# Reordering the operands, gates and reads of the output block products in a hybrid encoder layer

## The chip, the cores and the metric

The kernel runs on one core of a Trainium2 chip. The metric is the time on the device in microseconds (us), the median of several runs; less is better. The core has five engines with queues of their own: TensorE (PE, matrix products; PEld is its loading of weights), VectorE (DVE), ScalarE (ACT), GpSimd (POOL), and SyncE (SP), which issues most of the DMAs. Each engine works through its queue in order; between engines there are semaphores.

## What is computed

One layer of an encoder over 2048 tokens of width 1024, in float32. An input projection feeds two mixers: gated linear attention and latent attention with softmax, each with an output of width 512. What matters here is the end:

```python
    o_a = gla_branch(...)                       # (2048, 512), gated
    o_b = mla_branch(...)                       # (2048, 512), ends in o * silu(gate)
    mixed = concatenate([o_a, o_b], -1) @ w_out # (2048, 1024)
    x = layer_norm(ALPHA * x + mixed, ln_g, ln_b)
```

## The kernel before

Every product of float32 matrices is made of three matmuls (`mm3`, line 445): each operand is split into a high part, a copy rounded by ScalarE (`hi`, L393), and a low part, the difference, subtracted by GpSimd or VectorE (`lo`, L399). So each operand tile costs one ScalarE copy and one subtraction before TensorE can use it; the third matmul of a group is the first to need the low part.

The stages follow one another: the input projection with the linear attention, then softmax attention in 16 blocks (4 heads by 4 blocks of 512 queries), then the output projection of 16 chunks of 128 tokens. The tail of the attention is interleaved with chunks 0 to 5. The last attention block's output is made at the very end of that: TensorE's product `y` (L1802) in the bank "o" of PSUM, the copy `yc` of it to SBUF by ScalarE (L1807), and a store to DRAM (L1808); `rows` (L1784) copies and stores the reciprocals of the softmax sums.

Chunks 6 and 7 are plain products (8 k-tiles by 2 halves by 3, 48 matmuls each). Chunk 7 writes to the banks "o" and "ap". Chunks 8 to 15 are taken in four **pairs** of row blocks with seven block products instead of eight (class `Pair`, L1966): the activations of two chunks form the four blocks A11, A12 (row 0) and A21, A22 (row 1), and sums of them S1 = A21 + A22, S3 = A11 - A21, S2 = S1 - A11, S4 = A12 - S2. S2 and S4 overwrite A11, S3 overwrites A21, so S2 must wait until the split of A11 is done. The products are P1 (A11), P5 (S1), P6 (S2), P3 (S4), P7 (S3), P2 (A12), P4 (A22), twelve matmuls each, in this order on four PSUM banks 0, 1, 2, 3, 0, 1, 3; the last pair has P2 ahead of P7 and P4 in two halves. The second factors of P5 to P7 and, from the pairs on, of P4 are sums of blocks of w_out that were stored earlier and are fetched by `fetch_t` ("1h" to "4l"); "4h" and "4l" are four loads each (L2209).

The steps of a pair, each with its engine:

- `load` (L1979, SyncE): four DMAs per row: the linear attention's output to `of[:, 0]`, the gate and the softmax reciprocals to the buffer `gr`, the softmax attention's output to `of[:, 1]`. There is one buffer `gr` for even and one for odd chunks, shared by all pairs. Odd pairs take the two SBUF tiles `lng` and `lnb` as `of`, which held the norm's weights until `ln_psum` (L2196) has copied them to PSUM; even pairs take tiles "xf".
- `load_res` (L1994, SyncE): the residual row from `x`.
- `gate` (L1999, GpSimd): two multiplications per row, on the softmax half (A12 of row 0, A22 of row 1).
- `add` (L2007, VectorE), `hi` (ScalarE), `lo` (GpSimd): the operands.
- `copy` c1, c7 (ScalarE, L2036) and `sum` U2, U3 (VectorE, L2040): P1, and later P7, added to bank 2.
- `read` (VectorE, L2043): R1, R5, R5b, R2, R6, R3, R7, R4, R4b add banks to the two output rows; a product's bank is free for the next one after its reads.
- for row 0 `squares` and `scale` (ScalarE) and `centre` (VectorE, L2079, waits for the squares); for row 1 `stats` and `finish_a` (VectorE, with `rsqrt` on ScalarE); then `finish_b` for both (VectorE L2328, and the stores L2329). In the last pair row 0 ends on ScalarE and GpSimd (`finish_first`), which reads `lnbc`, a copy of the norm's bias (`copy_lnb`, L2083, ScalarE).

The order is written out by hand. `Pair.put` gives each step a place in time; the places are sorted, and `in_order` chains the instructions of all five engines in that sorted order. The places stand in `PLACE_PAIR` (L135), relative to T, the planned start of the pair's first product: T = 21.76 + 19.05 p for pair p, on a clock that begins with chunk 6. `load`, `res` and `gate` hold values for rows 0 and 1. `read_last` holds the last pair's places. The tables `put(place, fn)` of chunks 6 and 7, of `rows` (6.5), `yc` (6.51), `ln_psum` (2.0 and 3.5) and of `fetch_t` (1.0; 21.9 and 21.91) stand in `attention` (L1939 to L1963). So a step is moved past another by a change of its place alone, on its engine's queue only.

Of the kernel before, what the change touches and what calls it, by code (L numbers as in the profile page):

```python
# [80 lines left out]
    max=1.21,  # L81
    sub=(9.47, 8.65, 7.39, 7.37, 7.49, 6.63, 6.95, 7.44),
    exp=(10.18, 9.95, 7.63, 9.15, 8.26, 9.12, 7.84, 8.01),
    hi=(10.39, 10.41, 9.81, 10.32, 9.82, 10.74, 10.53, 10.47),
    lo=(11.99, 11.22, 11.21, 12.62, 11.98, 11.51, 10.87, 10.63),
# [22 lines left out]
    hi=(10.43, 11.83, 12.21, 14.39, 15.18, 22.96, 28.7, 34.03),  # L108
    lo=(15.35, 16.07, 20.38, 20.41, 24.45, 25.82, 33.5, 36.25),
# [9 lines left out]
    gate=(-20.72, -12.46, -4.41, 43.92),  # L119
# [14 lines left out]
PAIR0, PAIR_US = 8, 19.05  # L134
PLACE_PAIR = dict(  # L135
    load=(-31.0, -31.5),
    res=(-10.0, -8.0),
    gate=((-19.94, -18.58), (-24.72, -21.3)),
    add=dict(S1=-10.55, S3=-9.85, S2=-9.15, S4=-4.37),
    hi=dict(A11=-17.26, S1=-9.75, S2=-8.35, A12=-5.39, S3=-4.77, S4=-3.53, A22=-2.66),  # L140
    lo=dict(A11=-13.14, S1=-8.45, S2=-7.09, S3=-3.67, A22=1.77, A12=3.13, S4=4.49),
    product=dict(P1=0.0, P5=2.72, P6=5.44, P3=8.16, P7=10.88, P2=13.6, P4=16.32),
    last=dict(P1=0.0, P5=2.72, P6=5.44, P3=8.16, P2=10.88, P7=13.6, P4=16.32),
    gate1=((-14.6, -13.3), (-19.95, -18.6)),
    read=dict(c1=2.78, R1=5.9, R5=6.5, R5b=7.1, U2=10.61, R2=11.24, R6=11.87, c7=14.91, U3=15.63, R3=16.26, bn22=16.89,
              R7=17.52, sq=18.25, R4=20.34, R4b=20.97, bn21=21.6, rs=21.9, fa=(21.7, 22.23), fb=(23.9, 26.7)),
    read_last=dict(c1=2.78, lnb=3.5, R1=5.0, R5=6.3, R5b=6.9, U2=8.9, R2=9.5, R3=10.1, R4b=10.7, R6=11.5, bn12=12.1,
                   R7=14.1, bn11=14.7, R3p=16.9, R4p=17.5, bn22=18.1, fa=(15.3, 20.2), fb=(17.0, 20.3)),
)

# [61 lines left out]
    lo=(-0.5, 0.357),  # L212
# [79 lines left out]
    lo=(-0.452, -1.813),  # L292
# [65 lines left out]
    lo=(-0.124, 0.045),  # L358
# [24 lines left out]
class K:  # L383
# [819 lines left out]
    def sweep_c(self):  # L1203


        with ExitStack() as ctx:
# [17 lines left out]
            for n in SETUP_C:  # L1224
                put(n, 0, getattr(self, "su_" + n))
            for s in steps:
                for n in range(8):
                    put("pz", s["st"], self.c_pz, s, n, j=n)
                for n in STEP_C:
                    put(n, s["st"], getattr(self, "c_" + n), s)  # L1230
# [735 lines left out]
class Pair:  # L1966
# [128 lines left out]
    def put(self, put, T, last):  # L2095
        at = lambda place, fn, *a: put(T + place, fn, *a)
        P_, op = PLACE_PAIR, self.op
        if self.p:
            for r in (1, 0):
                at(max(P_["load"][r], 4.9 - T if self.p == 1 else -99) - 0.01 * r, self.load, r)  # L2100
        for r in range(2):
            at(P_["res"][r], self.load_res, r)
            for n in range(2):
                at(P_["gate1" if self.p == 1 else "gate"][r][n], self.gate, r, n)
        for n in self.OPERANDS:
            if n[0] == "S":
                at(P_["add"][n], self.add, n)
            at(P_["hi"][n], self.hi, n)
            at(-2.2 if n == "S4" and not self.p else P_["lo"][n], self.lo, n)
        bank = [lambda i=i: op.pw[i] for i in range(4)]  # L2110
        t = P_["last" if last else "product"]
        b = dict(P1=0, P5=1, P6=2, P3=3, P7=1 if last else 0, P2=0 if last else 1, P4=3)
        for n in t:
            if not (last and n == "P4"):
                at(t[n], self.product, n, bank[b[n]])
        e = P_["read_last" if last else "read"]
        at(e["c1"], self.copy, bank[0])
        at(e["U2"], self.sum, bank[2])
        if last:
            reads = (("R1", 0, 0, 0), ("R5", 1, 1, 1), ("R5b", 0, 1, 1), ("R2", 0, 1, 2), ("R3", 1, 1, 2), ("R4b", 1, 0, 2),  # L2120
                     ("R6", 0, 1, 3), ("R7", 0, 0, b["P2"]), ("R3p", 1, 1, b["P7"]), ("R4p", 1, 0, b["P7"]))
        else:
            at(e["c7"], self.copy, bank[b["P7"]])
            at(e["U3"], self.sum, bank[2])
            reads = (("R1", 0, 0, 0), ("R5", 1, 1, 1), ("R5b", 0, 1, 1), ("R2", 0, 1, 2), ("R6", 0, 1, 3), ("R3", 1, 1, 2),
                     ("R7", 0, 0, b["P2"]), ("R4", 1, 0, 3), ("R4b", 1, 0, 2))
        for n, r, h, x in reads:
            at(e[n], self.read, r, h, bank[x])
        if not last:
            at(e["bn22"], self.stats, 1, 1, 1)  # L2130
            at(e["bn21"], self.stats, 1, 0, 0)
            at(e["sq"], self.squares, 0)
            at(e["rs"], self.scale, 0)
            at(e["fa"][0], self.centre, 0)
            at(e["fa"][1], op.finish_a, self.rows[1])
            for r in range(2):
                at(e["fb"][r], op.finish_b, self.rows[r])
            return
        at(e["lnb"], self.copy_lnb)
        at(e["bn12"], self.stats, 0, 1, 1)  # L2140
        at(e["bn11"], self.stats, 0, 0, 0)
        at(e["bn22"], self.stats, 1, 1, 2, 3)
        for i, x in enumerate((3, 0)):
            cs, half = slice(256 * i, 256 * i + 256), lambda x=x: bank[x]()[:, :256]
            at(t["P4"] + PAIR_US / 14 * i, self.product, "P4", half, cs)
            at(t["P4"] + PAIR_US / 14 * (i + 1) + 0.45, self.read, 1, 0, half, cs)
            at(t["P4"] + PAIR_US / 14 * (i + 1) + 0.46, self.stats, 1, 0, i, 3, cs)
        at(e["fa"][0], op.finish_a, self.rows[0])
        at(e["fb"][0], self.finish_first)
        at(e["fa"][1], op.finish_a, self.rows[1])  # L2150
        at(e["fb"][1], op.finish_b, self.rows[1])
# [246 lines left out]
```

## Time and profile before

| | us |
|---|---|
| median of 3 runs | 1290.94 |
| the runs | 1290.94, 1289.06, 1290.98 |
| the profiled execution | 1290.68 |
| its span, first to last instruction | 1288.9 |
| outside of the span | 1.8 |

| engine | busy us | share of the span |
|---|---|---|
| PE | 1257.7 | 98% |
| DVE | 949.8 | 74% |
| ACT | 873.8 | 68% |
| POOL | 847.7 | 66% |

Times in rows of the profile are counted from the start of the span. A timeline row reads: start, duration, engine, line of the program, operation, tiles out<-in, shapes, count; in brackets the idle time of the engine ahead of it and what ended it. TensorE's rows overlap: a matmul begins before the one ahead of it has left the array, so the step from start to start is its price, not the duration. A row of a stretch (windows) reads: the stretch, its length, the busy time of PE, PEld, DVE, ACT and POOL with the number of instructions, the granted TensorE clock as a share of full speed, the mean share of time that the 16 DMA engines worked, and GB/s. Chunk 6 and 7 and the four pairs fill the stretch from 1172 us to the end.

### The profile page before, as it was taken

How to read it: one execution, taken by the hardware profiler on the slowest of the kernel's cores; microseconds unless marked ns; L12 is line 12 of the kernel's file. 1: busy time of each engine (PE TensorE's matmuls, PEld its weight loads, DVE VectorE, ACT ScalarE, POOL GpSimd, SP SyncE). 2: the span in 40 equal slices, each digit the busy share in tenths (PEclk: the TensorE clock that was granted, in tenths of full speed). 3: DMA queues.
4: the chain of work that ended last, by engine and by line, in shares of the span. 5: the costliest groups of instructions: out<-in, count | busy, mean ns of one | idle time of the engine just before them, and what ended most of it. 6: DMA issues, size and time to landing. Idle time of an engine off the chain costs nothing.

```text
span 1288.9 us, 20174 instructions
## 1 busy us (share of the span) xinstructions
PE 1257.7 (98%) x6928; PEld 1109.6 (86%) x6928; DVE 949.8 (74%) x1706; ACT 873.8 (68%) x1549; POOL 847.7 (66%) x546
## 2 busy tenths in 40 slices
PE   7999999999999999999999999999999999998996
PEld 7999999999889999999788888888888888887875
DVE  7865775555675455555798888888888889558897
ACT  7765657666676656655688888888888888623444
POOL 0245555453567666671288888889999999955771
PEclk9999999999999999999999999999999999999999
DMA  8332525253665565565501111122223212468951
GB/s 297 99 91 62 182 69 172 83 154 100 212 228 179 179 208 181 188 211 167 146 1 41 42 42 41 42 58 58 61 69 103 55 42 73 156 186 313 326 196 66
DMA packets 122518, 166.81 MB, mean 129 GB/s; under 512 B 18502, under 2 KB 71118, under 8 KB 121776
## 3 DMA queue, kind: packets, MB, share of 16 engines
q1 hardware_dynamic: 114256, 163.39, 39.9%
q0 software_dynamic: 768, 2.10, 0.5%
q8 instruction: 55, 0.90, 0.3%
q10 hardware_dynamic: 7392, 0.03, 0.3%
q14 instruction: 47, 0.39, 0.2%
HBM read 106.72 MB, written 58.75 MB: 128 GB/s over the span
## 4 chain that ended last, share of the span: by engine, by line
PE 75%; DVE 6%; ACT 5%; DMA 4%; POOL 3%; issue 2%; SPq 0%; DVEq 0%; POOLq 0%; ACTq 0%
PE o L447 4%; PE o L448 4%; PE o L449 4%; PE pS L1633 4%; PE pS L1634 4%; PE pS L1635 4%; PE pS L1636 4%; PE pS L1637 4%; PE ipa L447 3%; PE ipa L449 3%; PE ipa L448 3%; PE pz L448 2%; PE pz L449 2%; PE pz L447 2%; PE ipg L447 2%
## 5 line engine op out<-in xcount | busy, mean ns | idle before, releaser
L399 POOL TENSOR_TENSOR pl<-s,ph 128x1024 fp32r<-128x1024 f32 x128 | 306.4, 2418 | 56.3 <-ACT ph L393 56.3
L1655 DVE TENSOR_TENSOR rm<-pS,rm 128x512 f32<-128x512 f32 x210 | 144.8, 690 | 26.5 <-ACT s L1642 20.9
L1679 DVE TENSOR_TENSOR s<-s,mb 128x1024 f32<-128x1024 f32 x128 | 151.2, 1213 | 9.4 <-PE mb L1673 9.3
L1642 ACT ACTIVATE s<-pS 128x1024 f32<-128x1024 f32 x128 | 131.3, 1026 | 37.7 <-PE pS L1637 33.3
L393 ACT ACTIVATE ph<-s 128x1024 fp32r<-128x1024 f32 x128 | 135.0, 1057 | 13.5 <-PE o L449 12.9
L1683 ACT ACTIVATE s<-s 128x1024 f32<-128x1024 f32 x128 | 131.5, 1051 | 13.4 <-DVE s L1679 13.3
L447 PE MATMUL ipa<-wah,xah 128*128 128x384 f32 (+1 forms) x384 | 130.0, 338 | 6.5 <-ACT wah L393 6.5
L1096 POOL TENSOR_TENSOR Us<-Us,cw 128x512 f32<-128x512 f32 x16 | 18.6, 1164 | 173.7 <-DVE Us L1094 158.2
L449 PE MATMUL ipa<-wah,xal 128*128 128x384 f32 (+1 forms) x384 | 124.8, 325 | 0.0
L448 PE MATMUL ipa<-wal,xah 128*128 128x384 f32 (+1 forms) x384 | 124.5, 324 | 0.2 <-DVE wal L399 0.2
L1633 PE MATMUL pS<-qh,ckvT_h 128*128 128x512 f32 x256 | 102.7, 401 | 1.0 <-ACT s L1683 0.4
L447 PE MATMUL o<-ph,vh 128*128 128x512 f32 x256 | 101.1, 395 | 0.0
L1634 PE MATMUL pS<-ql,ckvT_h 128*128 128x512 f32 x256 | 99.9, 390 | 0.0
L1635 PE MATMUL pS<-qh,ckvT_l 128*128 128x512 f32 x256 | 99.9, 390 | 0.0
L1636 PE MATMUL pS<-rh,krs 128*128 128x512 f32 x256 | 99.8, 390 | 0.0
L449 PE MATMUL o<-ph,vl 128*128 128x512 f32 x256 | 99.8, 390 | 0.0
L1637 PE MATMUL pS<-rl,krs 128*128 128x512 f32 x256 | 99.8, 390 | 0.0
L448 PE MATMUL o<-pl,vh 128*128 128x512 f32 x256 | 99.7, 390 | 0.0
L1706 DVE TENSOR_TENSOR ap<-ap,s 128x512 f32<-128x512 f32 x120 | 83.1, 693 | 3.5 <-ACT s L1683 0.9
L447 PEld LDWEIGHTS ipa<-wah,xah 128*128 128x128 f32 x384 | 73.1, 190 | 7.4 <-ACT wah L393 6.8
L447 PE MATMUL pz<-xch,wzh 128*128 128x256 f32 x256 | 74.8, 292 | 0.0
L448 PEld LDWEIGHTS ipa<-wal,xah 128*128 128x128 f32 x384 | 73.1, 190 | 1.2 <-DVE wal L399 0.6
(446 smaller groups left out, 3906.0 us busy)
## 6 DMA issues: line engine op xcount, KB each, us to landing
xcf<-xT_dram SPq DMA_DIRECT2D x16, 512.0 KB, 5.7
xr<-x_dram SPq DMA_DIRECT2D x16, 512.0 KB, 6.2
xaf<-xT_dram SPq DMA_DIRECT2D x14, 512.0 KB, 3.8
wb<-wO_dram SPq DMA_DIRECT2D x16, 256.0 KB, 2.9
oib<-oi_s SPq DMA_DIRECT2D x16, 256.0 KB, 4.3
qdb<-qd_s SPq DMA_DIRECT2D x16, 256.0 KB, 4.3
SU<-su_s SPq DMA_DIRECT2D x16, 256.0 KB, 4.9
ub<-u_s SPq DMA_DIRECT2D x16, 256.0 KB, 4.2
```

Source lines behind the costliest of these rows:

```text
L393: return nc.scalar.activation(dst, src, AF.Copy).ins
L399: return e.tensor_tensor(dst, src, hi.bitcast(F32), ALU.subtract).ins
L447: mm(out, ah, bh, start=start, stop=False)
L448: mm(out, ah, bl, start=False, stop=False)
L449: mm(out, al, bh, start=False, stop=stop)
L1633: mm(ps[:, e], kh, qh, start=True, stop=False)
L1634: mm(ps[:, e], kh, ql, start=False, stop=False)
L1635: mm(ps[:, e], kl, qh, start=False, stop=False)
L1636: mm(ps[:, e], kr, rh, start=False, stop=False)
L1637: mm(ps[:, e], kr, rl, start=False, stop=True)
L1655: V.tensor_tensor(d["rm"], src[:, e], d["rm"], ALU.max)
L1679: V.tensor_tensor(s, s, d["mb"][:, None, :].to_broadcast([P, 2, QB]), ALU.subtract)
```

## The change

Only places are changed, and the few lines of `Pair.put` that look them up. Nothing is computed otherwise. In words:

- Pair 0: A11's high part goes from 4.50 to 6.56 on the common clock, behind `rows` (6.5) and `yc` (6.51). S3's high part goes ahead of S2's, S3's low part behind S2's and ahead of the gates of row 0; these gates (`gate0`) go from 1.82 and 3.18 to 15.76 and 17.06, behind the low parts of A11, S1, S2 and S3. A12's high part goes behind A22's. S4's low part stays.
- Pair 1: row 1's load goes from 9.3 to 4.91, ahead of `rows` and `yc` on SyncE; row 0's from 9.81 to 17.21, behind the residual loads of pair 0 (11.76, 13.76) and the stores of chunk 6 (15.88), ahead of "4h" (21.9).
- All pairs: the S2 add, and its high and low part, go about 1 us later, the reads U2 and R2 of the pair before 0.7 us sooner, so that on VectorE U2 and R2 stand ahead of the next pair's S2 add. The centring of row 0 goes from 21.7 to 22.9, behind `finish_a` of row 1 (22.23).
- Last pair: `lnbc` from 3.5 to 9.0, behind both `finish_b` of the pair before (4.85 and 7.65); R1 from 5.0 to 3.3, ahead of the first of them.

```diff
 PLACE_PAIR = dict(
     load=(-31.0, -31.5),
+    load1=(-23.6, -35.9),
     res=(-10.0, -8.0),
     gate=((-19.94, -18.58), (-24.72, -21.3)),
-    add=dict(S1=-10.55, S3=-9.85, S2=-9.15, S4=-4.37),
-    hi=dict(A11=-17.26, S1=-9.75, S2=-8.35, A12=-5.39, S3=-4.77, S4=-3.53, A22=-2.66),
-    lo=dict(A11=-13.14, S1=-8.45, S2=-7.09, S3=-3.67, A22=1.77, A12=3.13, S4=4.49),
+    add=dict(S1=-10.55, S3=-9.85, S2=-8.0, S4=-4.37),
+    hi=dict(A11=-17.26, S1=-9.75, S2=-7.3, A12=-5.39, S3=-4.77, S4=-3.53, A22=-2.66),
+    lo=dict(A11=-13.14, S1=-8.45, S2=-6.6, S3=-3.67, A22=1.77, A12=3.13, S4=4.49),
...
     gate1=((-14.6, -13.3), (-19.95, -18.6)),
-    read=dict(c1=2.78, R1=5.9, R5=6.5, R5b=7.1, U2=10.61, R2=11.24, R6=11.87, ...
-              R7=17.52, sq=18.25, R4=20.34, R4b=20.97, bn21=21.6, rs=21.9, fa=(21.7, 22.23), fb=(23.9, 26.7)),
-    read_last=dict(c1=2.78, lnb=3.5, R1=5.0, R5=6.3, ...
+    gate0=((-6.0, -4.7), (-24.72, -21.3)),
+    first=dict(hA11=-15.2, hS3=-8.0, hA12=-2.6, lS3=-6.5, lS4=-2.2),
+    read=dict(c1=2.78, R1=5.9, R5=6.5, R5b=7.1, U2=9.9, R2=10.5, R6=11.87, ...
+              R7=17.52, sq=18.25, R4=20.34, R4b=20.97, bn21=21.6, rs=21.9, fa=(22.9, 22.23), fb=(23.9, 26.7)),
+    read_last=dict(c1=2.78, lnb=9.0, R1=3.3, R5=6.3, ...
...
     def put(self, put, T, last):
         at = lambda place, fn, *a: put(T + place, fn, *a)
         P_, op = PLACE_PAIR, self.op
+        first = {} if self.p else P_["first"]
         if self.p:
             for r in (1, 0):
-                at(max(P_["load"][r], 4.9 - T if self.p == 1 else -99) - 0.01 * r, self.load, r)
+                at(P_["load1" if self.p == 1 else "load"][r], self.load, r)
         for r in range(2):
             at(P_["res"][r], self.load_res, r)
             for n in range(2):
-                at(P_["gate1" if self.p == 1 else "gate"][r][n], self.gate, r, n)
+                at(P_[f"gate{self.p}" if self.p < 2 else "gate"][r][n], self.gate, r, n)
         for n in self.OPERANDS:
             if n[0] == "S":
                 at(P_["add"][n], self.add, n)
-            at(P_["hi"][n], self.hi, n)
-            at(-2.2 if n == "S4" and not self.p else P_["lo"][n], self.lo, n)
+            at(first.get(f"h{n}", P_["hi"][n]), self.hi, n)
+            at(first.get(f"l{n}", P_["lo"][n]), self.lo, n)
```

More of the change, by code (lines that the diff above doesn't have):

```diff
@@ L144 @@
     gate1=((-14.6, -13.3), (-19.95, -18.6)),
-    read=dict(c1=2.78, R1=5.9, R5=6.5, R5b=7.1, U2=10.61, R2=11.24, R6=11.87, c7=14.91, U3=15.63, R3=16.26, bn22=16.89,
-              R7=17.52, sq=18.25, R4=20.34, R4b=20.97, bn21=21.6, rs=21.9, fa=(21.7, 22.23), fb=(23.9, 26.7)),
-    read_last=dict(c1=2.78, lnb=3.5, R1=5.0, R5=6.3, R5b=6.9, U2=8.9, R2=9.5, R3=10.1, R4b=10.7, R6=11.5, bn12=12.1,
+    gate0=((-6.0, -4.7), (-24.72, -21.3)),
+    first=dict(hA11=-15.2, hS3=-8.0, hA12=-2.6, lS3=-6.5, lS4=-2.2),
+    read=dict(c1=2.78, R1=5.9, R5=6.5, R5b=7.1, U2=9.9, R2=10.5, R6=11.87, c7=14.91, U3=15.63, R3=16.26, bn22=16.89,
+              R7=17.52, sq=18.25, R4=20.34, R4b=20.97, bn21=21.6, rs=21.9, fa=(22.9, 22.23), fb=(23.9, 26.7)),
+    read_last=dict(c1=2.78, lnb=9.0, R1=3.3, R5=6.3, R5b=6.9, U2=8.9, R2=9.5, R3=10.1, R4b=10.7, R6=11.5, bn12=12.1,
                    R7=14.1, bn11=14.7, R3p=16.9, R4p=17.5, bn22=18.1, fa=(15.3, 20.2), fb=(17.0, 20.3)),
```

## The prediction, made before the changed kernel ran

> **What bounds the kernel now.** I read the page first, then TensorE in order of time over the last 130 us, then what each gap waits for, then the other engines and the DMA in the same stretch.
>
> ```profile
> span 1288.9 us, 20174 instructions
> PE 1257.7 (98%) x6928; PEld 1109.6 (86%) x6928; DVE 949.8 (74%) x1706; ACT 873.8 (68%) x1549; POOL 847.7 (66%) x546
> ```
>
> TensorE is busy 98% of the span, so a reordering can only win its few gaps and the tail behind its last matmul. The change touches only what runs after 1173 us. There, in the timeline of TensorE (start, duration, line, tiles; a wait in brackets):
>
> ```profile
> 1161.61 0.39 PE L449 MATMUL po<-woh,ol 128*128 128x512 f32 x1
> ...
> 1172.04 0.39 PE L447 MATMUL pmb<-woh,oh 128*128 128x512 f32 x1
> ...
> 1183.58 0.39 PE L449 MATMUL px<-woh,ol 128*128 128x512 f32 x1
> 1187.39 0.62 PE L447 MATMUL po<-woh,oh 128*128 128x512 f32 x1 [3.42 <-ACT yc L1807]
> ...
> 1191.14 0.40 PE L447 MATMUL po<-woh,oh 128*128 128x512 f32 x1
> ...
> 1227.45 0.39 PE L448 MATMUL pw<-wol,S4h 128*128 128x512 f32 x1
> 1228.24 0.50 PE L449 MATMUL pw<-woh,S4l 128*128 128x512 f32 x1 [0.40 <-POOL S4l L399]
> 1228.57 0.39 PE L447 MATMUL pw<-woh,S4h 128*128 128x512 f32 x1
> ...
> 1254.89 0.39 PE L449 MATMUL pw<-woh,A12l 128*128 128x512 f32 x1
> 1255.28 0.47 PE L447 MATMUL pw<-woh,A22h 128*128 128x512 f32 x1
> 1255.59 0.40 PE L448 MATMUL pw<-wol,A22h 128*128 128x512 f32 x1
> ...
> 1268.78 0.39 PE L449 MATMUL pw<-woh,S4l 128*128 128x512 f32 x1
> 1269.60 0.50 PE L447 MATMUL pw<-woh,A12h 128*128 128x512 f32 x1 [0.43 <-DVE xr L2048]
> 1269.93 0.39 PE L448 MATMUL pw<-wol,A12h 128*128 128x512 f32 x1
> ...
> 1278.16 0.28 PE L449 MATMUL pw<-woh,A22l 128*128 128x256 f32 x1
> ```
>
> The first two rows are 46 steps apart: 10.43 / 46 = 0.227 us a matmul, 84 x 0.227 = 19.04 us for a pair of row blocks. Against that step the losses are: ahead of chunk 7, 1187.39 - 1183.58 - 0.227 = 3.58 us; then nine steps in 3.75 us instead of 2.04, 1.71 us; at product P3 of pair 1, 0.56 + 0.10 = 0.66; at 1255.28, 0.16 + 0.08 = 0.25; at 1269.60, 0.59 + 0.10 = 0.69. The last matmul ends at 1278.44, and 10.5 us follow it.
>
> The slow nine steps are the clock:
>
> ```profile
> 1183.90:1187.30 3.40, 0.07 (x1) 0.00 (x0) 3.25 (x5) 1.45 (x4) 1.89 (x2) 1.00 0.71 218
> 1187.30:1190.70 3.40, 3.31 (x8) 2.62 (x9) 3.12 (x7) 2.00 (x8) 0.46 (x1) 0.55 0.89 301
> ...
> 225.00:229.00 4.00, 3.36 (x24) 3.36 (x25) 2.42 (x5) 2.37 (x6) 0.00 (x0) 1.00 0.59 154
> ```
>
> (columns: stretch, length, busy time of PE, PEld, DVE, ACT, POOL, granted clock, DMA share, GB/s.) After 3.42 us of idling the granted clock was 0.55; the third row holds an idle of 1.08 us at 225.64, and there it stayed 1.00:
>
> ```profile
> 225.64 0.39 PE L448 MATMUL Ap<-qbl,kh 128*128 128x256 f32 x1 [1.08 <-DVE qbl L399]
> ```
>
> **The change part by part.** The copy ahead of the split, on ScalarE:
>
> ```profile
> 1183.11 1.01 ACT L2199 ACTIVATE ln<-lnb 128x1024 f32<-128x1024 f32 x1
> 1186.08 0.63 ACT L393 ACTIVATE A11h<-of 128x512 fp32r<-128x512 f32 x1 [1.95 <-DMA of<-oa_s]
> ...
> 1186.77 0.57 ACT L1807 ACTIVATE yc<-y 128x512 f32<-128x512 f32 x1
> ```
>
> The copy yc frees the bank of chunk 7; it stands behind a split that waits for a DMA. Put ahead, rt and yc follow the copy that ends at 1184.12: 0.57 for yc and a tenth for rt, done near 1184.8. The split still starts when its DMA lands, so it loses nothing. The gap shrinks from 3.58 to about 1.0 us, near the 1.08 us row that kept its clock. TensorE then leads by 2.56 + 1.71 = **4.3 us**, if nothing holds it later.
>
> It is held, at P3 of pair 1, by the low part S4l. GpSimd and the DMA queue:
>
> ```profile
> 1211.62 1.28 POOL L399 TENSOR_TENSOR S1l<-s,S1h 128x512 fp32r<-128x512 f32 x1
> ...
> 1218.00 1.30 POOL L2001 TENSOR_TENSOR of<-of,gr 128x512 f32<-128x512 f32 x1 [2.50 <-DMA of<-ob_s]
> 1219.25 1.30 POOL L399 TENSOR_TENSOR S3l<-lnb,S3h 128x512 fp32r<-128x512 f32 x1
> 1220.51 3.92 POOL L2001 TENSOR_TENSOR of<-of,gr 128x512 f32<-128x512 f32 x3
> 1224.39 1.30 POOL L399 TENSOR_TENSOR A22l<-lnb,A22h 128x512 fp32r<-128x512 f32 x1
> ...
> 1226.90 1.29 POOL L399 TENSOR_TENSOR S4l<-lng,S4h 128x512 fp32r<-128x512 f32 x1
> ```
>
> ```profile
> 1194.01 0.51 SPq L1989 DMA_DIRECT2D lng<-oa_s  x1
> ...
> 1211.96 0.53 SPq L1992 DMA_DIRECT2D of<-ob_s  x1
> ```
>
> ```profile
> 1188.00:1218.00 30.00, 30.00 (x128) 24.63 (x127) 23.52 (x33) 11.39 (x27) 21.09 (x17) 0.95 1.04 348
> ```
>
> GpSimd's order is written out: the first gate of pair 2 stands ahead of four low parts of pair 1, and waits for a load that was issued at 1211.96 and lands at 1218.0. From there eight operations end in S4l at 1228.19, 10.2 us after the landing. The change moves none of these eight. Nor can the load land much sooner: from 1188 to 1218 the 16 DMA engines are full (share 1.04), and the same transfers stand ahead of it. The edit load1 only swaps them: row 1 of pair 1 goes ahead of the stores of rt and yc (four issues), row 0 behind the two residual loads and the two stores of chunk 6, ahead of the fourth set of weights. Nothing is added or dropped. I give S4l 0 to 0.5 us and take **0.3**. TensorE comes to it at 1227.68 - 4.3 = 1223.4 instead, and waits until 1227.9. So the lead of 4.3 us is spent there, and the edits to pair 0 (S3l ahead of the gates, four low parts of about 1.3 us on GpSimd sooner) end at the same wait. They are costed at nothing; what hides them is that wait, with some 4 us of room.
>
> What remains is VectorE, which is late when TensorE ends:
>
> ```profile
> 1211.69 1.76 DVE L2013 TENSOR_TENSOR lng<-s,lng 128x512 f32<-128x512 f32 x1 [1.18 <-POOL A11l L399]
> 1213.38 0.69 DVE L2041 TENSOR_TENSOR pw<-pw,pc 128x512 f32<-128x512 f32 x1
> ...
> 1242.20 1.28 DVE L2081 SCALAR_TENSOR_TENSOR xr<-xr,nm,ln 128x1024 f32<-128x1024 f32 x1 [0.96 <-ACT wv_lq L2070]
> ...
> 1259.40 0.68 DVE L2048 SCALAR_TENSOR_TENSOR xr<-xr,pw 128x512 f32<-128x512 f32 x1
> ...
> 1262.50 1.28 DVE L2081 SCALAR_TENSOR_TENSOR xr<-xr,nm,ln 128x1024 f32<-128x1024 f32 x1 [0.96 <-ACT wv_lq L2070]
> ...
> 1267.54 1.40 DVE L2328 SCALAR_TENSOR_TENSOR xr<-xr,ln_r,ln 128x512 f32<-128x512 f32 x2 [2.14 <-ACT lnbc L2085]
> ...
> 1281.48 0.41 DVE L2050 TENSOR_TENSOR xr<-pw,xr 128x256 f32<-128x256 f32 x1
> ```
>
> The two centrings are 20.30 us apart, against TensorE's 19.04: VectorE falls back 1.26 us a pair. Three edits shorten it. U2 and R2 go ahead of the S2 add: that add takes 1.76 us while GpSimd makes S1l (from 1211.62, above), the U2 sum behind it 0.69; with 1.4 us of U2 and R2 ahead, S1l is over, and the add should take 0.69: 1.07 us a pair. The Trainium skill, "SBUF — State Buffer", section "Who interferes with whom", says that a VectorE instruction with two SBUF inputs is blocked for the whole of a GpSimd instruction that reads SBUF; the 1.76 agrees. The centring goes behind finish_a, 1.7 us of work that needs nothing from ScalarE: 0.96 us. So 20.30 - 2.03 = 18.3 us, under 19.04, and the lateness isn't built. In the last pair the copy lnbc moves from 3.5 to 9.0, behind the finish_b that waits 2.14 us for it; R1 goes ahead of that finish_b and needs only P1, the first product. From 1259.40 to the last read at 1281.48 are 22.1 us; less 0.96 and 2.14, 19.0: no more than TensorE's pair. The last read then follows the last matmul by some 0.2 us instead of 1281.48 - 1278.44 = 3.04: **2.8 us**. TensorE's waits at 1255.28 and 1269.60, for banks that VectorE reads late, go too: **0.25 + 0.69**.
>
> Behind the last read everything is as before. Sum: 0.3 + 0.25 + 0.69 + 2.8 = **4.0 us**. The profiled execution took 1290.68, 0.26 below the median of 1290.94; from the median, 1286.9.
>
> Unknown costs. The new gap at P3 is 4.5 us less 0.39 of matmul, at most 4.1 us of idling (up to 0.7 less if R6, behind the S2 add, holds P4 of pair 0). Half clock behind it costs 0 (the 1.08 us row) to 1.7 (the 3.42 us row); by length it is nearer to the second, but the runs of before, 1289.06 beside 1290.94 and 1290.98, differ by 1.9, as if a run could escape it after the same gap. So I keep both ends and take 0. The VectorE edits: 0 to 2.8, if new collisions eat them. The DMA: a landing up to 4 us sooner would bring all of the lead.
>
> **The rivals.**
> - *Half clock at the new gap*: the wait only moves from chunk 7 to P3 of pair 1, and is as long. 1286.9 + 1.7 = 1288.6. For it: 3.42 us gave 0.55. Against: the run of 1289.06. The Trainium skill, "TensorE: Matmul & The Clock Gate", Part 1, gives an idle window of about 3.4 us that runs free of the kernel; by that rule a gap of 4 us is caught in some runs only, and the trace agrees so far as it had 0.55 for one such stretch.
> - *The load lands early*, and S4l is no bound: 4.27 + 0.66 + 0.25 + 0.69 + 2.8 = 8.7 us, 1282.3; part of the way for each us sooner. Against: DMA share 1.04.
> - *Slower: SyncE is held.* Row 0 of pair 1 writes the gate buffer that row 0 of pair 0 still reads, and these gates now stand behind S2l and S3l. While SyncE waits there, the weights and pair 2's loads wait behind it. Worked from A11h's end at 1186.71 and four low parts with the S2 add between, the gates end near 1198, 4 us after 1194.01, where that load began before; loads take some 6 us to land, so the DMA has work for about that long. From 1200 on each us falls on S4l; to be 2.6 us slower than before, the gates must end near 1207: 1293.6.
> - *The reorder brings VectorE nothing*: the S2 add meets another operation of GpSimd and finish_a waits instead. Only 0.3 is left: 1290.6. Likewise, if yc were early without freeing chunk 7, the lead would be missing, and the sum still 4.0.
>
> **How the numbers follow.** Chances: the forecast 0.34 (1286.9, own range 1286 to 1288), half clock 0.30, early landing in whole or part 0.20, VectorE unmoved 0.08, SyncE held 0.08. A measurement here tells 0.2%, 2.6 us, from no change: below 1288.4 is faster. That is the forecast, the early landing and some two fifths of half clock: 0.66. Within: the rest of half clock and VectorE unmoved, 0.26. Slower: 0.08. The range from 1282.3 to 1290.0 leaves out SyncE held, VectorE unmoved and a sliver of the early landing.
>
> **What would show it.** Right: chunk 7 starts about 1 us late at clock 1.00; a wait of 3 to 4.5 us for S4l near 1223; the first gate of pair 2 near 1217.7; the S2 adds at 0.69; the last read within 0.5 us of the last matmul. Wrong: S4l with no wait (landing early), 1.7 us adds, SyncE idle at the row 0 load, or VectorE still 2 us behind at the end.

## The result and the profile after

| | before | after |
|---|---|---|
| median (runs) | 1290.30 us (8) | 1286.78 us (8) |
| lowest and highest run | 1288.27 to 1291.61 | 1285.95 to 1287.37 |
| profiled execution | 1290.68 | 1286.29 |
| its span | 1288.9 | 1284.5 |

The ratio of the times is 0.9974, with a 95% interval of 0.9963 to 0.9985: faster, by 1.9 to 4.8 us. The forecast of 1286.9 was 0.1 us off. How it came about is another matter: the sum was right, most of its terms were not, and that they nearly cancel was luck. Of the runs told of further below, one each of e5_s4 and e6_s4_finish took over 1700 us; these two are left out of the ratios.

Where rows of the two kernels are set side by side, one offset has to go first. The last matmul of chunk 6 begins at 1183.58 in the profiled execution of before and at 1182.88 in that of after. So 0.70 of the 4.4 us between the spans stand ahead of the change, and 3.7 us are its own.

The page of after, its span and the busy times:

```profile
span 1284.5 us, 20176 instructions
...
PE 1257.6 (98%) x6928; PEld 1110.4 (86%) x6928; DVE 941.5 (73%) x1706; ACT 874.0 (68%) x1549; POOL 846.9 (66%) x546
```

No engine does less work, but VectorE's busy time is 8.3 us shorter with the same number of instructions. TensorE in order of time:

```profile
1182.88 0.39 PE L452 MATMUL px<-woh,ol 128*128 128x512 f32 x1
1183.13 0.50 PE L450 MATMUL po<-woh,oh 128*128 128x512 f32 x1
...
1212.57 0.55 PE L450 MATMUL pw<-woh,A22h 128*128 128x512 f32 x1 [1.94 <-DVE xr L2053]
1212.91 0.63 PE L451 MATMUL pw<-wol,A22h 128*128 128x512 f32 x1
...
1225.70 0.50 PE L452 MATMUL pw<-woh,S4l 128*128 128x512 f32 x1
...
1274.62 0.28 PE L452 MATMUL pw<-woh,A22l 128*128 128x256 f32 x1
```

The wait ahead of chunk 7 is gone: 0.25 us from px to po, where a step is 0.227. A new wait stands at P4 of pair 0 (A22), for the read R6, and the stretch behind it is at half clock:

```profile
1209.50:1212.90 3.40, 1.46 (x6) 0.88 (x6) 2.34 (x2) 0.95 (x2) 2.11 (x3) 1.00 1.06 350
1212.90:1216.30 3.40, 3.40 (x9) 2.64 (x8) 2.26 (x4) 2.35 (x5) 1.89 (x2) 0.50 1.09 308
```

GpSimd and VectorE tell why R6 is late:

```profile
1205.80 3.08 POOL L2004 TENSOR_TENSOR lng<-lng,gr 128x512 f32<-128x512 f32 x2 [1.65 <-DMA lng<-ob_s]
1208.84 1.29 POOL L402 TENSOR_TENSOR A11l<-lng,A11h 128x512 fp32r<-128x512 f32 x1
...
1215.45 1.29 POOL L2004 TENSOR_TENSOR of<-of,gr 128x512 f32<-128x512 f32 x1 [1.51 <-DMA of<-ob_s]
...
1224.35 1.30 POOL L402 TENSOR_TENSOR S4l<-lng,S4h 128x512 fp32r<-128x512 f32 x1
```

```profile
1210.17 1.74 DVE L2016 TENSOR_TENSOR lng<-s,lng 128x512 f32<-128x512 f32 x1 [2.47 <-POOL A11l L402]
1211.83 0.68 DVE L2053 TENSOR_TENSOR xr<-pw,xr 128x512 f32<-128x512 f32 x1
```

The gates of pair 1 wait for a load, A11l stands behind them, the S2 add of pair 1 waits for A11l, R6 of pair 0 stands behind that add on VectorE, and P4 needs the bank that R6 frees. S4l, which was to hold TensorE, is ready at about the time it is wanted (1225.70; the step ahead of it is 0.06 us too long).

VectorE in the steady pairs, and then in the last one:

```profile
1219.40 0.21 DVE L2312 BATCH_NORM_AGGREGATE mv<-bn 128x2 f32<-128x12 f32 x1
...
1223.43 1.41 DVE L2332 SCALAR_TENSOR_TENSOR xr<-xr,ln_r,ln 128x512 f32<-128x512 f32 x2 [1.13 <-ACT ln_r L2326]
...
1230.53 0.68 DVE L2016 TENSOR_TENSOR of<-s,of 128x512 f32<-128x512 f32 x1
...
1233.29 1.76 DVE L2016 TENSOR_TENSOR of<-of 128x512 f32<-128x512 f32 x1 [1.48 <-POOL S2l L402]
...
1239.78 0.21 DVE L2312 BATCH_NORM_AGGREGATE mv<-bn 128x2 f32<-128x12 f32 x1
...
1258.00 0.68 DVE L2051 SCALAR_TENSOR_TENSOR xr<-xr,pw 128x512 f32<-128x512 f32 x1
...
1262.39 1.27 DVE L2084 SCALAR_TENSOR_TENSOR xr<-xr,nm,ln 128x1024 f32<-128x1024 f32 x1
1263.77 1.40 DVE L2332 SCALAR_TENSOR_TENSOR xr<-xr,ln_r,ln 128x512 f32<-128x512 f32 x2
...
1277.10 0.41 DVE L2053 TENSOR_TENSOR xr<-pw,xr 128x256 f32<-128x256 f32 x1
```

The S2 add takes 0.68 us as forecast in pairs 2 and 3; in pair 1 it still takes 1.74. But a pair still takes 1239.78 - 1219.40 = 20.38 us, because two other waits have come: 1.48 us for S2l ahead of the S4 add, and 1.13 us for ln_r at finish_b. In the last pair the two waits of before (0.96 and 2.14 us) are gone with nothing in their place: from the same read (1259.40 before, 1258.00 here) to the last read it is now 19.10 us, where it was 1281.48 - 1259.40 = 22.08. The last read begins 1277.10 - 1274.90 = 2.20 us behind the last matmul's end (3.04 before).

So VectorE, not TensorE, still brings up the end. Seen from it, the gain is 2.98 us in its last pair and 0.70 us (1259.40 - 0.70 - 1258.00) in everything ahead of that: 3.68 us. TensorE's end came 1278.44 - 0.70 - 1274.90 = 2.84 us sooner, but nothing waited for that.

### The profile page after: what moved, and what is told of

Read it like the earlier page. It is cut to its first block, busy times and chain, and to the rows that moved or that the text cites. A ratio compares the mean times of both kernels' runs of the same rounds, so it can differ in the third digit from the quotient of the medians.

```text
span 1284.5 us, 20176 instructions
## 1 busy us (share of the span) xinstructions
PE 1257.6 (98%) x6928; PEld 1110.4 (86%) x6928; DVE 941.5 (73%) x1706; ACT 874.0 (68%) x1549; POOL 846.9 (66%) x546
## 4 chain that ended last, share of the span: by engine, by line
PE 56%; POOL 4%; issue 3%; DMA 3%; DVE 3%; ACT 3%; SPq 0%; DVEq 0%; POOLq 0%; ACTq 0%
PE pS L1636 4%; PE o L452 4%; PE o L450 4%; PE o L451 4%; PE pS L1637 4%; PE pS L1638 4%; PE pS L1639 4%; PE pS L1640 4%; PE pz L451 2%; PE pz L452 2%; PE pz L450 2%; PE ipm L452 1%; PE ipm L450 1%; PE ipm L451 1%; PE po L451 1%
## 5 line engine op out<-in xcount | busy, mean ns | idle before, releaser
L452 PE MATMUL ipa<-wah,xal 128*128 128x384 f32 (+1 forms) x384 | 125.2, 326 | 0.0
L452 PE MATMUL o<-ph,vl 128*128 128x512 f32 x256 | 99.8, 390 | 0.0
```

Of the source, the lines that this page charges most:

```text
L452: mm(out, al, bh, start=False, stop=stop)
```

## The experiments

Each kernel was timed beside the kernel before on the same chip, four kernels to a chip. Two columns are from the profiled execution of each: the stage, from the start of chunk 6's last matmul to the start of the last read, and how far that read is behind the end of the last matmul.

| kernel | median us (runs) | ratio to before, 95% interval | stage us | behind us |
|---|---|---|---|---|
| before | | | 97.90 | 3.04 |
| after | 1286.78 (8) | 0.9974 (0.9963 to 0.9985) | 94.22 | 2.20 |
| e1_copy | 1290.16 (11) | 1.0007 (0.9998 to 1.0016) | 98.11 | 3.05 |
| e2_vector | 1287.34 (11) | 0.9985 (0.9977 to 0.9994) | 94.06 | 1.51 |
| e3_front | 1290.72 (12) | 1.0009 (0.9999 to 1.0020) | 100.30 | 3.04 |
| e4_read | 1287.37 (10) | 0.9987 (0.9978 to 0.9996) | 95.57 | 2.10 |
| after_again | 1287.31 (11) | 0.9982 (0.9973 to 0.9991) | 94.87 | 2.21 |
| e5_s4 | 1286.22 (10) | 0.9973 (0.9963 to 0.9983) | 94.03 | 0.11 |
| e6_s4_finish | 1285.30 (5) | 0.9960 (0.9947 to 0.9974) | 93.30 | 0.11 |
| e7_all | 1284.02 (5) | 0.9958 (0.9946 to 0.9971) | 92.95 | 0.59 |
| e8_lnb | 1287.42 (10) | 0.9977 (0.9968 to 0.9986) | 96.58 | 1.80 |
| e9_u2 | 1289.63 (11) | 0.9994 (0.9985 to 1.0002) | 98.02 | 3.04 |
| e10_centre | 1289.66 (11) | 0.9996 (0.9987 to 1.0006) | 97.47 | 3.04 |
| e11_c7 | 1283.63 (5) | 0.9945 (0.9932 to 0.9957) | 91.70 | 0.62 |

A profiled execution can lie apart from its kernel's median: that of e3_front took 1294.44 us, the longest of its twelve, that of e8_lnb 1289.35, the longest of its ten. The median of before was 1289.06 beside the first four, 1289.56 beside the next four and 1290.06 beside the last four.

### The change in two halves

**e1_copy**, the kernel before with the copy ahead of the split and nothing else:

```diff
-            at(P_["hi"][n], self.hi, n)
+            at(-15.2 if n == "A11" and not self.p else P_["hi"][n], self.hi, n)
```

> The copy yc ahead of the first split alone, everything else as before. Theory A (the lead that TensorE wins there is held later by VectorE and by S4l, whose load lands when the DMA allows): the gap of 3.6 us ahead of chunk 7 and its half clock go, a wait of 2 to 5 us comes up by P3 of pair 1, and the time is 1289 to 1291, within 1.3 us of before. Rival B (the copy is what the change lives on): 1286 to 1287.5, the whole gain of 3.5 us.

**e3_front**, the changed kernel with VectorE's edits and those to the last pair undone:

```diff
-    add=dict(S1=-10.55, S3=-9.85, S2=-8.0, S4=-4.37),
+    add=dict(S1=-10.55, S3=-9.85, S2=-9.15, S4=-4.37),
...
-    read=dict(... U2=9.9, R2=10.5, ... fa=(22.9, 22.23), fb=(23.9, 26.7)),
+    read=dict(... U2=10.61, R2=11.24, ... fa=(21.7, 22.23), fb=(23.9, 26.7)),
-    read_last=dict(c1=2.78, lnb=9.0, R1=3.3, ...
+    read_last=dict(c1=2.78, lnb=3.5, R1=5.0, ...
```

(The high and low part of S2 go back with its add.)

> The complement: the copy ahead, pair 0's splits and gates and pair 1's loads as in the change, VectorE's order and lnbc as before. Theory A: TensorE reaches pair 0 some 5 us sooner and loses it by P3 of pair 1; VectorE is 3 us late at the end as before; 1289 to 1290.5. Rival B: 1286 to 1287.5.

**e2_vector**, the other half alone: the kernel before with exactly the lines that e3_front takes out.

> Only the edits of VectorE's order and of lnbc: U2 and R2 ahead of the S2 add, centring behind finish_a, lnbc and R1 in the last pair; the copy, the gates of pair 0 and the loads of pair 1 as before. Theory A: the gap ahead of chunk 7 and its half clock stay, the wait for lnbc (2.1 us) goes, and most of the gain is here: 1287 to 1288.5. Rival B: no gain without the copy, 1289.5 to 1291.

The edits to the front alone bring nothing: 1.0007 and 1.0009, neither interval below 0.9998. VectorE's half brings 0.9985, which is not to be told from the whole change (0.9982 in after_again), and its stage of 94.06 us is that of the changed kernel (94.22). In e1_copy chunk 7 starts with 0.46 us of idling instead of 3.42, and the time comes back at P4 of pair 0, 3.26 us of wait with half clock behind it. In e3_front it is the same place, and the last pair's waits are as they were. TensorE and VectorE of e3_front:

```profile
1217.72 0.80 PE L450 MATMUL pw<-woh,A22h 128*128 128x512 f32 x1 [3.99 <-DVE xr L2053]
```

```profile
1266.28 1.28 DVE L2084 SCALAR_TENSOR_TENSOR xr<-xr,nm,ln 128x1024 f32<-128x1024 f32 x1 [0.96 <-ACT wv_lq L2073]
1271.32 1.41 DVE L2332 SCALAR_TENSOR_TENSOR xr<-xr,ln_r,ln 128x512 f32<-128x512 f32 x2 [2.14 <-ACT lnbc L2088]
```

In e2_vector the wait ahead of chunk 7 and its half clock stay (2.76 us), and from 1260.60 to the last read at 1279.70 VectorE takes 19.10 us, just what it takes in the changed kernel. What e1_copy and e3_front don't show by themselves is that a lead of TensorE would be worth nothing: TensorE had none left in them. Its last matmul ended 95.06 and 97.26 us behind the start of the stage (the stage less the last column of the table), 94.86 before.

### Which hold comes second: R6 or S4l

**e4_read**, the changed kernel with R6 of pair 0 ahead of the S2 add of pair 1:

```diff
         first = {} if self.p else P_["first"]
+        late = dict(aS2=-7.1, hS2=-6.95) if self.p == 1 else {}
...
-                at(P_["add"][n], self.add, n)
-            at(first.get(f"h{n}", P_["hi"][n]), self.hi, n)
+                at(late.get(f"a{n}", P_["add"][n]), self.add, n)
+            at(late.get(f"h{n}", first.get(f"h{n}", P_["hi"][n])), self.hi, n)
```

> The changed kernel with the S2 add of pair 1, and its high part, behind the read R6 of pair 0, which TensorE waited 1.94 us for in the changed kernel's profile. Theory A: that wait and the half clock behind it (together 3.8 us) go, and a wait of about 3.5 us for S4l appears at P3 of pair 1 instead: 1286 to 1287.5, as the changed kernel. Rival C (R6 is the place that decides): 1283 to 1285.

The wait at P4 of pair 0 is gone, and TensorE then stands where the prediction had it, at S4l. This is TensorE of e4_read:

```profile
1227.33 0.50 PE L452 MATMUL pw<-woh,S4l 128*128 128x512 f32 x1 [2.46 <-POOL S4l L402]
1227.66 0.40 PE L450 MATMUL pw<-woh,S4h 128*128 128x512 f32 x1
```

So the hold by S4l is real, and it was covered by the nearer one. The time can't be told from that of the changed kernel (0.9987 beside 0.9982). That fits with VectorE being behind at the end in both (2.10 and 2.21 us), whichever of the two holds TensorE.

**after_again**, the changed kernel once more, as a measure for the three kernels beside it.

> The changed kernel as it is, beside the next three on the same chip, so that they can be compared with it. Theory A and rival alike: 0.9965 to 0.9985 of before.

P4 of pair 0 waits 1.94 us as in the first profile, but here no half clock follows, and TensorE comes to S4l early enough to wait 1.57 us there. The time is the same within the interval.

### VectorE's period

**e5_s4**, the changed kernel with the S4 add of pairs 1 to 3, and its high part, behind U3 and R3 of the pair before:

```diff
+        late = dict(aS4=-2.75, hS4=-2.7) if self.p else {}
```

(`late` is looked up as in e4_read.)

> The changed kernel with the S4 add (and its high part) of pairs 1 to 3 behind the sum U3 and the read R3 of the pair before. Theory A (VectorE's chain still takes 20.4 us a pair in the changed kernel, because the S4 add waits 1.5 us for S2l and finish_b 1.1 us for ScalarE, and this sets the end): U3 and R3 fill the wait of 1.5 us, the distance of two finish_a falls from 20.4 to about 19, the last read comes 1 to 1.5 us closer to the last matmul (2.2 us in the changed kernel), 1 to 2.5 us less than the changed kernel. Rival D (VectorE's period does not set the end, only where TensorE was held): no difference, within 0.6 us of the changed kernel.

The S4 add has no wait any more. U3 has one in its place, 1.95 and 1.62 us for the copy c7. The last read now follows the last matmul within 0.11 us, so VectorE has caught up. But TensorE lost 2.02 us at S4l of pair 1 in this execution and half clock behind it, so of the 2.1 us of lag only 0.84 show in the stage (94.87 to 94.03).

**e6_s4_finish**, e5_s4 with finish_b of row 0 later, behind R1, R5 and R5b of the next pair:

```diff
-fb=(23.9, 26.7)
+fb=(26.3, 26.7)
```

> As the run before, and the first finish_b of a pair, which waits 1.1 us for ScalarE's ln_r, behind the next pair's reads R1, R5 and R5b. Theory A: the distance of two finish_a falls below TensorE's 19.0 plus its waits, VectorE waits for TensorE at the end, the last read within 0.6 us of the last matmul; 2 to 3 us less than the changed kernel. Rival D: within 0.6 us of it.

The wait of 1.13 us for ln_r is gone. VectorE of e6_s4_finish near the end of pair 2:

```profile
1252.79 0.70 DVE L2044 TENSOR_TENSOR pw<-pw,pc 128x512 f32<-128x512 f32 x1 [1.62 <-ACT pc L2041]
...
1256.83 0.69 DVE L2051 SCALAR_TENSOR_TENSOR xr<-xr,pw 128x512 f32<-128x512 f32 x1 [0.83 <-PE pw L452]
```

VectorE now waits for TensorE (0.83 us), and its pair 2 takes 19.04 us (the aggregates at 1239.97 and 1259.01): TensorE's own 19.04. Now TensorE is the bound that the prediction took it to be from the start. On the same chip the median went from 1287.31 (after_again) over 1286.22 to 1285.30 us. The intervals of neighbours overlap, and those of the first and the last still touch (0.9973 to 0.9991, 0.9947 to 0.9974), so the gain in time is likely and not clear; the waits and the lag in the trace are.

**e7_all**, e6_s4_finish with R6 ahead of the S2 add as in e4_read, and pair 2's gates behind pair 1's low parts:

```diff
+    gate2=((-13.85, -13.75), (-14.05, -13.95)),
...
-                at(P_[f"gate{self.p}" if self.p < 2 else "gate"][r][n], self.gate, r, n)
+                at(P_[f"gate{self.p}" if self.p < 3 else "gate"][r][n], self.gate, r, n)
```

> As the run before, and TensorE's lead set free: R6 of pair 0 ahead of pair 1's S2 add, and GpSimd's four gates of pair 2 behind pair 1's four low parts, so that S4l no longer waits for pair 2's loads. Theory A: no wait at P4 of pair 0 nor at P3 of pair 1 beyond 1 us, no half clock in the pairs, TensorE ends 3 to 4 us sooner, and with VectorE's shorter chain the whole takes 1281 to 1284 us, 4 to 6 us less than the changed kernel. Rival E (the DMA holds it whatever the order, through the loads of pair 2 and the residual rows): 1285 or more.

1284.02 us. Neither P4 of pair 0 nor S4l of pair 1 holds TensorE, and no stretch has half clock. TensorE's largest wait is now at the first product of pair 1:

```profile
1215.82 0.50 PE L451 MATMUL pw<-woh,A11h 128*128 128x512 f32 x1 [1.59 <-ACT pc L2042]
```

**e11_c7**, e7_all with the copy c7 of pair 0 ahead of the high parts S2h, A12h and S3h of pair 1, which it stood behind:

```diff
-            at(e["c7"], self.copy, bank[b["P7"]])
+            at(e["c7"] if self.p else 12.0, self.copy, bank[b["P7"]])
```

> The fastest kernel so far (all waits of the front moved) with ScalarE's copy c7 of pair 0 also ahead of the high parts S2h, A12h, S3h of pair 1. Theory A: TensorE's wait of 1.59 us for that copy at the first product of pair 1 goes and nothing ahead of the end takes it back, except for 0.2 to 0.6 us at later banks; 1.0 to 1.4 us less than the fastest kernel, so 1282.6 to 1283.0. Rival B: the first product of pair 1 then waits for something else (A11l, or a read of VectorE), or S4l does at product P3 as in the changed kernel: 1284.0, no gain.

1283.63 us, which lies between the two expectations. The wait for c7 is gone, and one of about the same size stands one product on, at P5, for a read of VectorE. TensorE of e11_c7:

```profile
1217.67 0.50 PE L451 MATMUL pw<-wt1h,S1h 128*128 128x512 f32 x1 [1.34 <-DVE xr L2054]
```

Its ratio of 0.9945 (0.9932 to 0.9957) and that of e7_all, 0.9958 (0.9946 to 0.9971), overlap; whether it is better than e7_all stays open. Both beat the changed kernel: e7_all beside after_again on the same chip (0.9973 to 0.9991), e11_c7 against both of its measurements, by intervals that don't touch.

### VectorE's three edits one by one

**e8_lnb**, the kernel before with two numbers changed:

```diff
-    read_last=dict(c1=2.78, lnb=3.5, R1=5.0, ...
+    read_last=dict(c1=2.78, lnb=9.0, R1=3.3, ...
```

> The kernel before, with the copy lnbc at 9.0 and R1 at 3.3 in the last pair and nothing else changed. Theory A: the 2.14 us wait in finish_b goes, but the copy now stands where it waits itself, and only what VectorE gained between the last finish_a and the last read in the run with all VectorE edits is won: 0.85 us, ratio near 0.9993, the last read 2.0 to 2.4 us behind the last matmul. Rival (the prediction's term): all 2.14 us are won, ratio near 0.9984, last read about 0.9 us behind.

0.9977 (0.9968 to 0.9986): two numbers of one line bring a gain that can't be told from that of the whole change (0.9974 and 0.9982). Which of the two brings how much was not run. VectorE of e8_lnb:

```profile
1260.31 0.68 DVE L2048 SCALAR_TENSOR_TENSOR xr<-xr,pw 128x512 f32<-128x512 f32 x1
...
1263.40 1.28 DVE L2081 SCALAR_TENSOR_TENSOR xr<-xr,nm,ln 128x1024 f32<-128x1024 f32 x1 [0.96 <-ACT wv_lq L2070]
...
1266.82 1.40 DVE L2328 SCALAR_TENSOR_TENSOR xr<-xr,ln_r,ln 128x512 f32<-128x512 f32 x2
...
1280.15 0.41 DVE L2050 TENSOR_TENSOR xr<-pw,xr 128x256 f32<-128x256 f32 x1
```

The wait of 0.96 us is still there, that of 2.14 us is gone from finish_b, and from the same read as above to the last one it is 1280.15 - 1260.31 = 19.84 us, 2.24 less than before. So the rival was right, and theory A, which expected 0.85, fell. Its 0.85 was misread: it counted from the aggregate of finish_a to the last read, but with VectorE's edits the centring (1.27 us) stands behind that aggregate and without them ahead of it, so two unlike stretches had been compared. In this execution 0.9 us of it were lost in pair 0, where VectorE waited 1.92 us for TensorE: behind the wait of 3.36 us ahead of chunk 7 half clock held for 14 steps, 6.12 us instead of 3.18, where it had held for nine before. So the last read is 1.80 us behind and not the 0.9 that the rival named; the median has the whole.

**e9_u2**, the kernel before with U2 and R2 ahead of the next pair's S2 add:

```diff
-    add=dict(S1=-10.55, S3=-9.85, S2=-9.15, S4=-4.37),
+    add=dict(S1=-10.55, S3=-9.85, S2=-8.0, S4=-4.37),
...
-    read=dict(c1=2.78, ... U2=10.61, R2=11.24, ...
+    read=dict(c1=2.78, ... U2=9.9, R2=10.5, ...
```

(S2's high and low part go along, to -7.3 and -6.6.)

> The kernel before, with U2 and R2 ahead of the next pair's S2 add in all pairs and nothing else changed. Theory A: U2 and R2 fill the wait for A11l once, in pair 0, and the S2 add's shorter time is given back by the S4 add: 0.5 to 1.0 us in all, ratio 0.9992 to 0.9996, finish_a still some 20.3 us apart. Rival (the prediction's term): 1.07 us a pair, three times, so finish_a 19.2 us apart, the last read within 0.3 us of the last matmul, ratio near 0.9978.

VectorE of e9_u2 at the adds of pair 3, and its finish_b in the last pair:

```profile
1252.79 0.68 DVE L2013 TENSOR_TENSOR lng<-s,lng 128x512 f32<-128x512 f32 x1
...
1255.54 1.75 DVE L2013 TENSOR_TENSOR lng<-lng 128x512 f32<-128x512 f32 x1 [1.47 <-POOL S2l L399]
...
1268.00 1.41 DVE L2328 SCALAR_TENSOR_TENSOR xr<-xr,ln_r,ln 128x512 f32<-128x512 f32 x2 [2.14 <-ACT lnbc L2085]
```

Theory A holds: the S2 add takes 0.68 us, the S4 add waits 1.47, the aggregates stay 20.38 us apart (1223.40, 1243.79, 1264.16). The ratio, 0.9994 (0.9985 to 1.0002), can't be told from no change.

**e10_centre**, the kernel before with the centring behind finish_a:

```diff
-              ... rs=21.9, fa=(21.7, 22.23), fb=(23.9, 26.7)),
+              ... rs=21.9, fa=(22.9, 22.23), fb=(23.9, 26.7)),
```

> The kernel before, with the centring of row 0 behind finish_a of row 1 and nothing else changed. Theory A: the wait of 0.96 us for ScalarE's squares goes and finish_b waits about 1.1 us for ScalarE's ln_r in its place: nothing won, ratio 0.9995 to 1.0005. Rival (the prediction's term): 0.96 us a pair, finish_a 19.3 us apart, ratio near 0.998.

VectorE of e10_centre, finish_b of pair 1's rows, then the last pair:

```profile
1245.57 1.41 DVE L2328 SCALAR_TENSOR_TENSOR xr<-xr,ln_r,ln 128x512 f32<-128x512 f32 x2 [1.09 <-ACT ln_r L2322]
...
1263.48 1.28 DVE L2081 SCALAR_TENSOR_TENSOR xr<-xr,nm,ln 128x1024 f32<-128x1024 f32 x1
1267.83 1.41 DVE L2328 SCALAR_TENSOR_TENSOR xr<-xr,ln_r,ln 128x512 f32<-128x512 f32 x2 [3.07 <-ACT lnbc L2085]
```

Theory A holds here too: the centring waits no more, and the next instruction waits for it, 1.09 us for ln_r and in the last pair 3.07 for lnbc, 0.93 more than the 2.14 of before. What the one edit sets free, the next wait takes, as long as lnbc is where it was.

## Why the prediction was right, and where it was not

1. *The copy ahead of the split: right.* 0.13 us lost ahead of chunk 7 (1182.88 to the second step behind, 1183.47, less two steps of 0.227), about 1.0 forecast, and full clock. So TensorE led by more than the 4.3 us of the sum, by 5.2.
2. *The lead is held at S4l of pair 1: wrong place.* It was held at P4 of pair 0, by R6: 2.33 - 0.23 = 2.10 us of wait from start to start, and 1.71 of half clock. I had R6 in the text as "up to 0.7 less", with the S2 add of pair 1 where it was before and at 0.69 us. R6 came near that: the add starts 0.82 us sooner and takes 1.74, and R6 ends at 1212.51 + 0.70 = 1213.21, where 1211.69 and twice 0.69 give 1213.07. What was off is what stands on both sides of it. TensorE of before at P4 of pair 0:

   ```profile
   1216.35 0.39 PE L447 MATMUL pw<-woh,A22h 128*128 128x512 f32 x1
   ```

   and TensorE of after at the matmul ahead of P4:

   ```profile
   1210.24 0.39 PE L452 MATMUL pw<-woh,A12l 128*128 128x512 f32 x1
   ```

   P4 was due a step behind this, at 1210.47 + 0.70 = 1211.17, 5.18 us sooner than before and not 4.3. And S4l ended at 1225.65 + 0.70 = 1226.35 instead of 1228.19, so after the 3.8 us lost at P4 nothing was left to wait for. e4_read shows that S4l holds TensorE once R6 doesn't.

   I also took load1 for a mere swap ("Nothing is added or dropped"). But it put row 0 of pair 1 later: in the eight profiled executions with it the last of this row's loads is issued 15.3 to 16.5 us behind the start of chunk 6's last matmul and the gates of pair 1 wait 1.65 to 3.63 us for it; in the six without it, it is issued at 12.5 to 13.7 us and the gates don't wait for it. Behind these gates stand A11l, the S2 add and R6. What the front would bring without load1 was not run.
3. *The load of pair 2: too small.* 0 to 0.5 us sooner was forecast; the first gate starts at 1215.45 + 0.70 = 1216.15 instead of 1218.00, 1.85 us. Its load is issued at 1209.42 instead of 1211.96, by the same offset 1.84 us sooner. The whole of it comes from the issue; the DMA's share of 1.04 said that the engines were full, not which transfers stood ahead. That load1 moved the issue is not shown: counted from the start of chunk 6's last matmul, it came at 26.54 and 27.33 us in the two executions of the changed kernel and at 28.76 in e3_front, which has the edit, and without it at 28.38 (before), 28.44 (e1_copy) and 27.07 (e2_vector).
4. *VectorE's period 20.30 to 18.3 us: wrong.* It measured 20.38. In pairs 2 and 3 the S2 add became 1.07 us shorter, and the centring stopped waiting, as forecast. But U2 and R2 had been filling the time in which S2h and S2l are made. VectorE of before, the S2 and the S4 add of pair 2:

```profile
1230.94 1.75 DVE L2013 TENSOR_TENSOR of<-s,of 128x512 f32<-128x512 f32 x1
...
1234.78 1.76 DVE L2013 TENSOR_TENSOR of<-of 128x512 f32<-128x512 f32 x1
```

   From the end of the one to the start of the other it is 1234.78 - 1232.69 = 2.09 us here, and 1233.29 - 1231.21 = 2.08 after; before it held U2, R2 and R6, now R6 and a wait of 1.48. The centring's 0.96 turned into 1.13 at finish_b, whose ln_r comes at the end of ScalarE's chain of six small instructions. The rival "the reorder brings VectorE nothing", at a chance of 0.08, had the kind of it (a wait that only moves), not the places.
5. *The last pair, 22.1 to 19.0 us: right.* 19.10. There lnbc's wait is gone and R1 stands where finish_b would have waited for ln_r, so both gains stay. e8_lnb shows that lnbc and R1 alone bring a gain like that of the whole change. e10_centre shows the centring worth nothing without them.
6. *The last read 0.2 us behind the last matmul: wrong*, 2.20; and TensorE's end, forecast 1.24 us sooner, came 2.84 sooner (its waits of 0.25 and 0.69 us went, as forecast, and 1.9 of the lead came through). The two errors, 2.0 us too late and 1.6 too early, nearly cancel. The sum of 4.0 stands against 3.68. That is luck, and so is a part of the 0.1 us: the forecast was taken from a median of 1290.94 over three runs; from the 1290.30 over eight, the same sum gives 1286.3.

Three of the signs that the forecast named for being wrong were there: S4l without a wait, an S2 add of 1.7 us (in pair 1), and VectorE 2.20 us behind at the end.

The step that failed behind 4 and 6 is the term "20.30 - 2.03 = 18.3 us": it took each wait that an edit removes as time won, without asking what VectorE would wait for next. Ahead of it stands the first sentence on the bound, "TensorE is busy 98% of the span, so a reordering can only win its few gaps and the tail behind its last matmul". VectorE had 3.04 us of lag at the end, and by these rows a gain of TensorE reaches the end only when that lag is gone. e1_copy and e3_front, which give TensorE its gap back and leave VectorE as it was, gained nothing, though TensorE lost its lead on the way there as well.

Of the rivals, half clock at the new gap came in one execution of the changed kernel and not in the other, at P4 of pair 0. SyncE was not held for long: its longest wait from 1183 to 1220 is 1.0 us.

Why VectorE has only 0.70 us more ahead of its last pair can be read but was not tested: its S2 add of pair 1 waits for A11l in both kernels and starts at 1210.17 + 0.70 = 1210.87 instead of 1211.69, 0.82 us sooner, and from there its period is the same. What sets A11l in the changed kernel is the landing of pair 1's load ahead of the gates. Nor is it shown that the 0.82 us come from the front: behind the start of chunk 6's last matmul the add starts at 27.29 and 27.90 us in the two executions of the changed kernel, at 28.11 in before, and at 27.14 in e2_vector, which has no edit of the front. Also not tried: the edits of e8_lnb with those of e5_s4 to e11_c7, but without the front.

## What to carry to other kernels

Ask which engine does the last thing, and follow its own waits back; a gap closed on the engine with 98% may bring nothing while another one is late behind it. When an instruction is moved out of a stretch, look what it was hiding there: a time from producer to consumer (here 2.08 us from the S2 add over ScalarE and GpSimd to the S4 add) stays, filled or not. When steps are moved behind others on one engine, follow the chain on through each engine until it meets the one whose lead is counted.

## What the runs showed of the hardware

Half clock followed idle times shorter than the 3.42 us of before, and not by length. TensorE of e9_u2 ahead of chunk 7, 2.86 us of idling and steps of 0.43 behind it:

```profile
1187.17 0.63 PE L447 MATMUL po<-woh,oh 128*128 128x512 f32 x1 [2.86 <-ACT yc L1807]
1187.61 0.63 PE L448 MATMUL po<-wol,oh 128*128 128x512 f32 x1
1188.03 0.63 PE L449 MATMUL po<-woh,ol 128*128 128x512 f32 x1
```

TensorE of e10_centre at the same place, 3.03 us and steps of 0.23:

```profile
1187.72 0.50 PE L447 MATMUL po<-woh,oh 128*128 128x512 f32 x1 [3.03 <-ACT yc L1807]
1188.06 0.40 PE L448 MATMUL po<-wol,oh 128*128 128x512 f32 x1
1188.29 0.39 PE L449 MATMUL po<-woh,ol 128*128 128x512 f32 x1
```

In the other profiled executions half clock followed 1.94 (after), 2.02 (e5_s4), 2.17 (e6_s4_finish), 2.76, 3.26, 3.36 and 3.99 us, and did not follow 1.57, 1.59, 1.66, 1.94 (after_again) and 2.46 (e4_read). The Trainium skill, "TensorE: Matmul & The Clock Gate", Part 1, has an idle window of about 3.4 us that runs free of the kernel. That 1.94 us was caught once and missed once agrees with a window that runs free of the kernel; that 1.94 us can be enough does not agree with its length. Nor is the price fixed: the steps at half clock lost 1.71 us in before and in after, 1.45 in e2_vector and 2.94 in e8_lnb. At such a place 1.5 to 2.9 us may come and go from run to run, which only many runs average out.
